# The remainder product of the attention scores: 64 partitions, or 128 with zeros in half of them

## The chip, the cores and the metric

The kernel runs on one core of a Trainium2 chip. What counts is the time of one execution on the device, in microseconds (us); lower is better. Before the change three executions took 495.58, 497.87 and 500.51 us, the median being 497.87 us.

## What is computed

One decoder layer in float32 on 256 tokens of 1024 channels. The part that matters here is the attention. There are two kinds, with heads of 64 channels: 12 dilated heads in three groups, and 8 block heads. For each head the scores are a product of queries and keys over the 64 channels of that head:

```python
sc = jnp.einsum('brhnqd,brhnkd->brhnqk', qb, kb).astype(jnp.float32) * scale   # dilated
s_own = jnp.einsum('bhqd,bhnd->bhqn', qc, ko).astype(jnp.float32) * scale      # block (256 tokens: one block)
p = softmax(masked scores);  o = p @ v
```

Around the attention stand large products with weights: an input projection of 1024 by 8448 columns, gates, branch projections, an output projection, and a feed-forward part of 2816 hidden channels. Two layer norms end the two halves.

## The kernel before

**Numbers in two parts.** TensorE multiplies float32 numbers here in a form that is rounded to fewer bits (`float32r`). Each operand is therefore split into a rounded part and a remainder, and a product is the sum of three matmuls: part by part, part by remainder, remainder by part (`mm3`, lines 198 to 202). The splitting is done by `split` (lines 148 to 150): ScalarE (ACT) casts, VectorE (DVE) subtracts. The weights go through it too: `prep` (line 129) takes pieces of 128x512 that a DMA has brought in and splits each, up to 10 pieces (`LEAD`) ahead of their use.

**The order.** The main thread is a run of projections. `project` (line 209) does two tiles of 128 channels, each a sum of 24 matmuls of 128x256 in a bank of PSUM. After each tile `tick` (line 155) splits further weights, takes the product out of its bank, and takes one entry from the list `side`. An entry of `side` is one stage of an attention: scores, exponentials, transposes, values. So TensorE meets a burst of score matmuls every few ticks between the matmuls of projections, and keeps its program order throughout.

**Queries and keys.** Heads go in pairs, head a of a pair at partitions 64a to 64a+63 of a tile. `queries` (line 233) stores for head a the rounded part on its own half of the partitions and the remainder on the other half, so that one tile of 128 partitions holds both. `keys` (line 244) stores the rounded part of the keys twice, once on each half (the tile `k`); a first matmul over 128 partitions then gives part by part plus remainder by part in one go (line 265). The remainder of the keys lies only on the head's own half (the tile `kl`, one for two pairs of heads, made at line 246 and filled at line 257). A second matmul over these 64 partitions (line 266) adds part by remainder to the same bank.

**How many.** A score is those two matmuls for one head and one tile of 128 queries by 256 keys. A dilated stage (`score`, line 316) does six scores, and there are four such stages. A block stage (`score`, line 360) does four, and there are four of these too. That makes 40 scores, 80 matmuls, in eight bursts. The DVE reads the finished scores at line 273, ACT takes the exponentials at line 275, DVE normalizes at line 280, and the results are transposed on TensorE at line 287.

**Buffers.** Nearly all tiles of 128x512 come from one pool with 61 slots (`buf`, line 57). GpSimd (POOL) does almost nothing: an iota at the start and four tiny powers in the layer norms.

Of the kernel before, what the change touches and what calls it, by code (L numbers as in the profile page):

```python
# [7 lines left out]
F32 = mybir.dt.float32  # L8
F32R = mybir.dt.float32r
# [5 lines left out]
P = 128  # L15
# [22 lines left out]
def trunk(ctx: ExitStack, tc, x, w_in, w_short_conv, w_moba_proj, w_dil_proj, w_conv_proj, w_mix_out,  # L38
# [26 lines left out]

    # ---- the stream of weights: blocks of up to [128, 2048] are loaded, and in pieces of 512 columns
    # ---- rounded to the tensor engine's 12-bit form, with the remainder
    blocks = []

    def block(*parts):  # L70
        """parts: DRAM access patterns [128, k, columns], one behind the other in the block"""
        blocks.append(parts)
# [56 lines left out]
    def prep(n=1):  # L129
        """the next n pieces, as far as they may run ahead"""  # L130
        for _ in range(n):
            i = len(ready)
            if i >= min(len(pieces), used[0] + LEAD):
                return
            r, c, last = pieces[i]
            h, l = buf(F32R), buf(F32R)
            split(r[:, c:c + 512], h, l)
            ready.append((h, l))
            if last:
                load_next()  # L140

    def take(n):
        """the next n pieces"""
        i = used[0]
        assert len(ready) >= i + n, (len(ready), i, n)
        return ready[i:i + n]
# [4 lines left out]

    # ---- work set between the products that hold the tensor engine
    side, late = [], []

    def tick(n, consume=None, ahead=1):
        """after n pieces' worth of products: what the last time left, more weights, what takes these
        products, and a stage of the work that is set between"""
        used[0] += n
        while late:
            late.pop(0)()  # L160
        prep(n + ahead)
        if consume:
            consume()
        if side:
            side.pop(0)()

    # ---- the tensor engine's clock is raised while the first loads are under way
    warm = const.tile([P, 512], BF16, name="warm")
# [4 lines left out]

    # ---- x, and its transpose
    xs = act.tile([P, 2, D], F32, tag="xs", name="xs", bufs=2)
# [20 lines left out]

    # ---- products
    def mm3(o, ah, al, bh, bl, first, last):
        """o += (ah + al)' (bh + bl), all but the product of the two remainders (2^-24)"""
        nc.tensor.matmul(o, ah, bh, start=first, stop=False)  # L200
        nc.tensor.matmul(o, ah, bl, start=False, stop=False)  # L201
        nc.tensor.matmul(o, al, bh, start=False, stop=last)  # L202

    def cut(w, k, c0, c1):
        """rows k, columns c0..c1 of a block of 256 columns in pieces w"""
        c = (k % 2) * 256
        return [t[:, c + c0:c + c1] for t in w[k // 2]]

    def project(consume, xh=xTh, xl=xTl, ahead=1):
        """[128 channels, 256 tokens] for two tiles of channels; consume(tile, product)"""  # L210
        w = take(4)
        for c in range(2):
            o = acc((P, T))
            for k in range(KT):
                mm3(o, *cut(w, k, c * P, c * P + P), xh[:, k, :], xl[:, k, :], k == 0, k == KT - 1)
            tick(2, lambda: consume(c, o), ahead)

    def project_tokens():
        """tokens by 256 channels, in two parts: [128 tokens, 2, 256 channels]"""
        w = take(4)  # L220
        vh, vl = buf(F32R, (P, 2, 256)), buf(F32R, (P, 2, 256))
        for t in range(2):
            s = slice(t * P, (t + 1) * P)
            o = acc((P, T))
            for k in range(KT):
                mm3(o, xTh[:, k, s], xTl[:, k, s], *cut(w, k, 0, 256), k == 0, k == KT - 1)
            tick(2, lambda: split(o, vh[:, t, :], vl[:, t, :]))
        return vh, vl

    # ---- attention: heads go in pairs, head a of a pair at partitions 64 a  # L230
    HALF = (slice(0, 64), slice(64, 128))

    def queries(store):
        """per tile of two heads: [part and remainder of a head, 2 heads, 256 tokens]"""
        def consume(c, o):
            q = buf(F32R, (P, 2, T))
            for a in range(2):
                s, n = HALF[a], HALF[1 - a]
                nc.scalar.copy(q[s, a, :], o[s, :])
                nc.vector.tensor_sub(q[n, a, :], o[s, :], q.bitcast(F32)[s, a, :])  # L240
            store.append(q)
        return consume

    def keys(store):
        """per tile: the part of a head, twice [128, 2 heads, 256 tokens]; the remainders [128, 256]"""
        kl = buf(F32R, (P, 2, T))

        def consume(c, o):
            k = buf(F32R, (P, 2, T))
            for a in range(2):  # L250
# [4 lines left out]
                else:  # L255
                    nc.vector.tensor_copy(k[n, a, :], o[s, :])
                nc.vector.tensor_sub(kl[s, c, :], o[s, :], k.bitcast(F32)[s, a, :])
            store.append((k, kl[:, c, :]))
        return consume

    def scores(o, q, k, a, t):
        """o [128 queries of tile t, 256 keys] for head a of a pair"""
        kd, kl = k
        ts = slice(t * P, (t + 1) * P)
        nc.tensor.matmul(o, q[:, a, ts], kd[:, a, :], start=True, stop=False)  # L265
        nc.tensor.matmul(o, q[HALF[a], a, ts], kl[HALF[a], :], start=False, stop=True)  # L266

    def exponentials(e, parts):
        """parts: (part of e, scores in PSUM, mask); e = exp((s + mask) / 8 - max); returns its sums"""
        n = len(parts)  # L270
# [11 lines left out]
    def turned(blks):  # L282
        """transposes of up to four [128, 128] tiles, split: two of [128, 4, 128]"""
        n = len(blks)
# [11 lines left out]
    def values(vs, ps, c):  # L296
        """vs: per group (vh, vl); ps: per group the transposed probabilities of keys 0..127 and 128..255"""
        o = att((P, 2, T))
# [13 lines left out]
    def dilated(c, dq, dk, dv, y):  # L312
        """the stages of a pair of heads, the three groups in one softmax"""
        es, ps, en = {}, {}, []
# [73 lines left out]

    # ---- masks (additive), by shape alone
    mask1 = const.tile([P, 3, 2, P], F32, name="mask1")  # L390
# [12 lines left out]

    # ---- small per-channel weights, turned to columns
    sconv = const.tile([P, 3, 4], F32, name="sconv")
# [22 lines left out]

    # ---- the mixer's projections and attention
    dq, dk, dv = [[], [], []], [[], [], []], []  # L430
# [71 lines left out]

    # ---- gates and branch projections
    merged = []
# [25 lines left out]

    # ---- layer norm
    half_c = const.tile([P, 1], F32, name="half_c")
    nc.vector.memset(half_c, -0.5)

    def residual(r, res, o, st, i, c0, c1):
        """columns c0..c1 of r = ALPHA res + o, with their statistics"""
        nc.vector.scalar_tensor_tensor(r[:, c0:c1], res[:, c0:c1], ALPHA, o, op0=OP.mult, op1=OP.add)
        nc.vector.bn_stats(st[:, i, :], r[:, c0:c1])

    def norm(r, st, gB, bB, ends, done=lambda c0, c1: None):  # L540
        """over r, in parts of columns that end at ends; done(first column, last)"""
        mv = act.tile([P, 4], F32, tag="mv", name=fresh("mv"), bufs=2)
# [11 lines left out]
    def row_products(o, a, w, k, t, c0, c1, first, last):  # L554
        """o += columns c0..c1 of row k of a block of 1024 columns, in pieces w, by the tokens of tile t"""
        ah, al = (v[:, k, t * P:(t + 1) * P] for v in a)
# [3 lines left out]
    def sums():  # L560
        """banks of the sums of the two token tiles by parts of the columns: (first column, last, sum)"""
        res = []
# [4 lines left out]
    def finish(o, t, parts, r, res, between=lambda: None):  # L567
        """the last products of token tile t, in parts of columns that end one after the other, and the
        residual sum; parts: (activations, pieces of the weights)"""
        st = act.tile([P, len(o), 6], F32, tag="bn", name=fresh("bn"), bufs=2)  # L570
# [12 lines left out]

    # ---- output projection of the mixer, tokens by channels
    x1 = act.tile([P, 2, D], F32, tag="xs", name="x1", bufs=2)
# [37 lines left out]

    # ---- gated feed-forward with a causal convolution
    def taps(v, o, ch):
# [5 lines left out]
    def hidden(j):  # L631
        """the consumers of the two halves of w_up, and what they give"""
        vg, vv = buf(F32, (P, 2, T)), buf(F32, (P, 2, T))
# [98 lines left out]
```

## Time and profile before

| what | value |
|---|---|
| time of three executions | 495.58, 497.87, 500.51 us |
| median | 497.87 us |
| span of the profiled execution, first to last instruction | 493.7 us |
| TensorE matmul busy | 483.7 us (98%) |
| VectorE busy | 361.6 us (73%) |
| ScalarE busy | 271.9 us (55%) |
| GpSimd busy | 4.3 us (1%) |

The profiled execution is another one than the three that were timed, and the only time that its records hold is its span of 493.7 us. The times of executions without the profiler stand 1.8 to 6.8 us above that span, the median 4.1 us. The timeline gives for each instruction its start and its duration. The matmuls overlap one another in a pipeline, so what one of them costs in a run of them is not its duration but the distance from its start to the start of the next.

### The profile page before, as it was taken

The numbers are of one execution on the slowest core, as the hardware profiler recorded it, in microseconds if no ns is written. First come the engines' busy times: TensorE is split into PE (matmuls) and PEld (weight loads), VectorE is DVE, ScalarE is ACT, GpSimd is POOL, SyncE is SP. The second block draws the span as 40 slices with busy tenths as digits, with TensorE's granted clock in tenths as the row PEclk, the third lists the DMA queues.
The fourth block names the chain that finished last, engine by engine and source line by source line (L and its number), as shares of the span: only waits on it lengthen the run. The fifth ranks groups of instructions, "written<-read, shape, count | busy, mean of one in ns | idle before, by whom it ended". The sixth has DMA issues, their size and how long they took to land.

```text
span 493.7 us, 9076 instructions
## 1 busy us (share of the span) xinstructions
PE 483.7 (98%) x3582; PEld 457.3 (93%) x3582; DVE 361.6 (73%) x775; ACT 271.9 (55%) x579; POOL 4.3 (1%) x9
## 2 busy tenths in 40 slices
PE   8999999999999999999999999999999999999993
PEld 5999788999899999999999889999999999999983
DVE  6888768476788865656565986798677867776966
ACT  4768455364756673535353712876655646565710
POOL 0000000000000000000000000000000000000000
PEclk9999899999999999999999999999999999999997
DMA  8975535353435163737374843546656374556102
GB/s 265 362 233 175 167 96 161 86 170 106 152 110 169 39 217 108 242 122 244 119 254 174 276 151 129 214 157 212 229 175 216 124 251 173 166 178 195 61 1 86
DMA packets 69502, 83.51 MB, mean 169 GB/s; under 512 B 1688, under 2 KB 64852, under 8 KB 69460
## 3 DMA queue, kind: packets, MB, share of 16 engines
q1 hardware_dynamic: 69460, 82.94, 51.4%
q8 instruction: 28, 0.46, 0.4%
q14 instruction: 14, 0.11, 0.1%
HBM read 81.89 MB, written 1.05 MB: 168 GB/s over the span
## 4 chain that ended last, share of the span: by engine, by line
PE 97%; DMA 1%; DVE 1%; SPq 0%; ACT 0%; issue 0%; DVEq 0%
PE acc L200 23%; PE acc L202 23%; PE acc L201 23%; PE att L200 6%; PE att L201 6%; PE att L202 6%; PE att L266 3%; PE att L265 2%; PE att L287 1%; PE acc L439 1%; DMA xs<-in_x_dram 1%; PE att L194 0%; DVE r L551 0%; SPq L124 0%; SPq L177 0%
## 5 line engine op out<-in xcount | busy, mean ns | idle before, releaser
L150 DVE TENSOR_TENSOR b<-raw,b 128x512 fp32r<-128x512 f32 x300 | 196.4, 686 | 39.6 <-ACT b L149 36.5
L149 ACT CAST b<-raw 128x512 fp32r<-128x512 f32 x300 | 169.6, 620 | 6.9 <-DMA raw<-in_w_in_dram 3.9
L200 PE MATMUL acc<-xTh,b 128*128 128x256 f32 x432 | 123.3, 285 | 0.0
L201 PE MATMUL acc<-xTl,b 128*128 128x256 f32 x432 | 122.2, 283 | 0.0
L202 PE MATMUL acc<-xTh,b 128*128 128x256 f32 x432 | 122.2, 283 | 0.0
L200 PE MATMUL acc<-x1Th,b 128*128 128x256 f32 x320 | 90.9, 284 | 0.0
L202 PE MATMUL acc<-x1Th,b 128*128 128x256 f32 x320 | 90.6, 283 | 0.0
L201 PE MATMUL acc<-x1Tl,b 128*128 128x256 f32 x320 | 90.5, 283 | 0.0
L200 PEld LDWEIGHTS acc<-xTh,b 128*128 128x128 f32 x432 | 82.8, 192 | 0.7
L201 PEld LDWEIGHTS acc<-xTl,b 128*128 128x128 f32 x432 | 82.8, 192 | 0.0
L202 PEld LDWEIGHTS acc<-xTh,b 128*128 128x128 f32 x432 | 82.8, 192 | 0.0
L201 PEld LDWEIGHTS acc<-x1Tl,b 128*128 128x128 f32 x320 | 61.4, 192 | 0.1
L200 PEld LDWEIGHTS acc<-x1Th,b 128*128 128x128 f32 x320 | 61.4, 192 | 0.1
L202 PEld LDWEIGHTS acc<-x1Th,b 128*128 128x128 f32 x320 | 61.4, 192 | 0.0
L629 DVE SCALAR_TENSOR_TENSOR b<-acc,fconv,b 128x255 f32<-128x255 f32 x80 | 38.4, 480 | 30.2 <-ACT b L627 29.2
L200 PE MATMUL att<-b,b 128*128 128x512 f32 (+1 forms) x170 | 58.9, 347 | 0.0
L201 PE MATMUL att<-b,b 128*128 128x512 f32 (+1 forms) x170 | 58.9, 347 | 0.0
L202 PE MATMUL att<-b,b 128*128 128x512 f32 (+1 forms) x170 | 58.7, 345 | 0.0
L149 ACT CAST b<-b 128x256 fp32r<-128x256 f32 x34 | 13.8, 408 | 47.3 <-DVE b L525 23.4
L627 ACT ACTIVATE b<-acc,fconv 128x256 f32<-128x256 f32 x40 | 22.6, 564 | 28.7 <-PE acc L202 28.6
L200 PEld LDWEIGHTS att<-b,b 128*128 128x128 f32 x170 | 32.2, 189 | 4.0
L202 PEld LDWEIGHTS att<-b,b 128*128 128x128 f32 x170 | 32.1, 189 | 4.0
(109 smaller groups left out, 646.6 us busy)
## 6 DMA issues: line engine op xcount, KB each, us to landing
raw<-in_w_in_dram SPq DMA_DIRECT2D x31, 1024.0 KB, 5.7
raw<-in_w_up_dram SPq DMA_DIRECT2D x22, 1024.0 KB, 5.1
raw<-in_w_down_dram SPq DMA_DIRECT2D x11, 1024.0 KB, 5.1
raw<-in_w_mix_out_dram SPq DMA_DIRECT2D x4, 1024.0 KB, 5.1
raw<-in_w_in_dram SPq DMA_DIRECT2D x8, 256.0 KB, 6.0
raw<-in_w_conv_proj_dram SPq DMA_DIRECT2D x4, 512.0 KB, 3.6
raw<-in_w_moba_proj_dram SPq DMA_DIRECT2D x4, 512.0 KB, 4.6
xs<-in_x_dram SPq DMA_DIRECT2D x4, 256.0 KB, 3.5
```

The costliest lines, as they stand in the source:

```text
L149: nc.scalar.copy(h, src)
L150: nc.vector.tensor_sub(l, src, h.bitcast(F32))
L200: nc.tensor.matmul(o, ah, bh, start=first, stop=False)
L201: nc.tensor.matmul(o, ah, bl, start=False, stop=False)
L202: nc.tensor.matmul(o, al, bh, start=False, stop=last)
L265: nc.tensor.matmul(o, q[:, a, ts], kd[:, a, :], start=True, stop=False)
L266: nc.tensor.matmul(o, q[HALF[a], a, ts], kl[HALF[a], :], start=False, stop=True)
L287: nc.tensor.transpose(p[:, i, :], b, ident)
L439: nc.tensor.matmul(o[c], w[i][:, s:s + P], xt[:, k, :], start=k + i == 0 and xt is xTh, stop=k == KT - 1 and i == 1)
L627: nc.scalar.activation(v, o, AF.Identity, bias=w[3], scale=w[0])
L629: nc.vector.scalar_tensor_tensor(v[:, j:], o[:, :T - j], w[j], v[:, j:], op0=OP.mult, op1=OP.add)
```

## The change

`keys` makes a tile of remainders for each pair of heads (`kl`, now inside `consume`) in the same layout as the tile of parts: for head a, the remainder lies on that head's half of the partitions, and GpSimd writes zeros on the other half. `scores` runs both matmuls over all 128 partitions with the same stationary operand. Over the zeros, the rows that hold the remainder of the queries add nothing. The rest of the diff takes comments and doc strings away, so the line numbers stay nearly the same.

```diff
     def keys(store):
-        """per tile: the part of a head, twice [128, 2 heads, 256 tokens]; the remainders [128, 256]"""
-        kl = buf(F32R, (P, 2, T))
+
 
         def consume(c, o):
-            k = buf(F32R, (P, 2, T))
+            k, kl = buf(F32R, (P, 2, T)), buf(F32R, (P, 2, T))
+            for a in range(2):
+                nc.gpsimd.memset(kl.bitcast(F32)[HALF[1 - a], a, :], 0.0)
             for a in range(2):
                 s, n = HALF[a], HALF[1 - a]
                 nc.scalar.copy(k[s, a, :], o[s, :])
@@ -254,19 +255,18 @@
                     nc.scalar.copy(k[n, a, :], o[s, :])
                 else:
                     nc.vector.tensor_copy(k[n, a, :], o[s, :])
-                nc.vector.tensor_sub(kl[s, c, :], o[s, :], k.bitcast(F32)[s, a, :])
-            store.append((k, kl[:, c, :]))
+                nc.vector.tensor_sub(kl[s, a, :], o[s, :], k.bitcast(F32)[s, a, :])
+            store.append((k, kl))
         return consume
 
     def scores(o, q, k, a, t):
-        """o [128 queries of tile t, 256 keys] for head a of a pair"""
-        kd, kl = k
-        ts = slice(t * P, (t + 1) * P)
-        nc.tensor.matmul(o, q[:, a, ts], kd[:, a, :], start=True, stop=False)
-        nc.tensor.matmul(o, q[HALF[a], a, ts], kl[HALF[a], :], start=False, stop=True)
+
+        qt = q[:, a, t * P:(t + 1) * P]
+        for i in range(2):
+            nc.tensor.matmul(o, qt, k[i][:, a, :], start=i == 0, stop=i == 1)
```

## Rows read from the trace of the kernel before

**Rows 1.** The page's first part: span, and for engines the busy time, share of the span and number of instructions.

```profile
span 493.7 us, 9076 instructions
...
PE 483.7 (98%) x3582; PEld 457.3 (93%) x3582; DVE 361.6 (73%) x775; ACT 271.9 (55%) x579; POOL 4.3 (1%) x9
```

**Rows 2.** The page's chain of work that ended last, followed back from the last instruction: shares of the span by engine, then by line.

```profile
PE 97%; DMA 1%; DVE 1%; SPq 0%; ACT 0%; issue 0%; DVEq 0%
PE acc L200 23%; PE acc L202 23%; PE acc L201 23%; PE att L200 6%; PE att L201 6%; PE att L202 6%; PE att L266 3%; PE att L265 2%; PE att L287 1%; PE acc L439 1%; DMA xs<-in_x_dram 1%; PE att L194 0%; DVE r L551 0%; SPq L124 0%; SPq L177 0%
```

**Rows 3.** The view of who waited for whom, PE alone: us in total, times, longest.

```profile
PE att L194 <- DMA xs<-in_x_dram: 1.2, 2, 0.8
PE acc L172 <- DVE warm L169: 1.2, 1, 1.2
```

**Rows 4.** The timeline of PE around the burst of four block scores at 126.56 us: start, duration, line, rows*columns of the array, shape of the moving operand.

```profile
126.20 0.28 PE L200 MATMUL acc<-xTh,b 128*128 128x256 f32 x1
126.33 0.28 PE L201 MATMUL acc<-xTl,b 128*128 128x256 f32 x1
126.44 0.28 PE L202 MATMUL acc<-xTh,b 128*128 128x256 f32 x1
126.56 0.28 PE L265 MATMUL att<-b,b 128*128 128x256 f32 x1
126.77 0.38 PE L266 MATMUL att<-b,b 64*128 64x256 f32 x1
127.08 0.39 PE L265 MATMUL att<-b,b 128*128 128x256 f32 x1
127.40 0.38 PE L266 MATMUL att<-b,b 64*128 64x256 f32 x1
...
128.65 0.38 PE L266 MATMUL att<-b,b 64*128 64x256 f32 x1
128.96 0.39 PE L200 MATMUL acc<-xTh,b 128*128 128x256 f32 x1
129.19 0.28 PE L201 MATMUL acc<-xTl,b 128*128 128x256 f32 x1
```

**Rows 5.** The timeline of PEld, the loads of the stationary operand, over the same burst.

```profile
126.45 0.19 PEld L265 LDWEIGHTS att<-b,b 128*128 128x128 f32 x1
126.77 0.18 PEld L266 LDWEIGHTS att<-b,b 64*128 64x128 f32 x1
127.08 0.19 PEld L265 LDWEIGHTS att<-b,b 128*128 128x128 f32 x1
```

**Rows 6.** The timeline of PE at the transposes of the small weights, with 12 and 44 rows.

```profile
33.23 0.44 PE L425 MATMUL att<-ident,b 44*128 44x44 f32 x4
33.61 0.39 PE L200 MATMUL acc<-xTh,b 128*128 128x256 f32 x1
33.83 0.28 PE L201 MATMUL acc<-xTl,b 128*128 128x256 f32 x1
```

**Rows 7.** Eight stretches, each from the first score matmul of a burst to the next matmul of a projection: the stretch and its length; busy time of PE (and how many instructions touch the stretch, those that began before it included), granted clock, DMA share, GB/s.

```profile
48.10:51.95 3.85, 3.85 (x15) 0.93 0.70 209
56.17:59.82 3.65, 3.65 (x14) 1.00 0.69 241
65.69:69.34 3.65, 3.65 (x15) 1.00 0.92 282
80.03:83.67 3.64, 3.64 (x15) 1.00 0.54 133
126.57:128.96 2.39, 2.39 (x10) 1.00 0.46 108
131.93:134.32 2.39, 2.39 (x10) 1.00 0.00 0
157.95:160.35 2.40, 2.40 (x11) 1.00 0.33 109
163.31:165.71 2.40, 2.40 (x11) 1.00 0.00 0
```

**Rows 8.** Stretches of 1 us at the end of the first burst and behind it: busy time of PE, PEld, DVE, ACT and POOL with their counts, granted clock (1.00 is 2.4 GHz, 0.50 is 1.2 GHz), DMA share, GB/s.

```profile
51.00:52.00 1.00, 1.00 (x4) 0.53 (x3) 0.97 (x5) 0.81 (x1) 0.00 (x0) 0.70 1.08 385
52.00:53.00 1.00, 1.00 (x6) 1.00 (x6) 0.91 (x4) 1.00 (x4) 0.00 (x0) 0.50 0.69 225
53.00:54.00 1.00, 1.00 (x6) 1.00 (x6) 0.88 (x2) 0.34 (x2) 0.00 (x0) 0.50 0.00 0
54.00:55.00 1.00, 1.00 (x8) 1.00 (x7) 0.00 (x0) 0.00 (x0) 0.00 (x0) 0.59 0.02 6
```

**Rows 9.** GpSimd's groups of instructions: shapes and count, busy time, mean ns of one.

```profile
L545 POOL TENSOR_TENSOR mv<-mv,half_c 128x1 f32<-128x1 f32 x4 | 3.8, 955 | 483.8 <-DVE mv L544 483.8
L183 POOL IOTA diff<- 128x128 int32 x1 | 0.2, 236 | 0.4 <-POOLq L719 0.4
L719 POOL MEMSET const-float32-0.0<- 128x1 f32 x1 | 0.1, 99 | 0.2 <-issue 0.2
```

**Rows 10.** Four longer stretches in the form of rows 8: the projections of the keys, the four dilated bursts, the stretch behind them, and the block attention.

```profile
30.00:48.00 18.00, 18.00 (x152) 17.79 (x151) 16.31 (x34) 13.70 (x32) 0.00 (x0) 1.00 0.61 185
48.00:84.00 36.00, 36.00 (x215) 29.71 (x214) 27.34 (x74) 19.73 (x45) 0.00 (x0) 0.95 0.45 134
84.00:120.00 36.00, 36.00 (x288) 35.22 (x287) 22.73 (x47) 17.33 (x39) 0.00 (x0) 1.00 0.42 130
120.00:180.00 60.00, 60.00 (x444) 55.35 (x443) 48.54 (x142) 39.32 (x103) 0.00 (x0) 1.00 0.38 120
```

**Rows 11.** The view of who waited for whom, the DVE's wait for finished scores.

```profile
DVE e L273 <- PE att L266: 7.2, 11, 2.3
```

**Rows 12.** The timeline of the DVE as it splits the last transposed probabilities of the first block stage.

```profile
139.79 0.42 DVE L150 TENSOR_TENSOR b<-att,b 128x256 fp32r<-128x256 f32 x1
```

**Rows 13.** The timeline of PE as it uses them in the values of that stage.

```profile
141.50 0.28 PE L200 MATMUL att<-b,b 128*128 128x256 f32 x1
141.62 0.28 PE L201 MATMUL att<-b,b 128*128 128x256 f32 x1
```

**Rows 14.** The timeline of the DVE in the projections of the keys: two pieces of weights split, and the subtractions that make the remainders of keys for the first pair of heads of the third group.

```profile
40.89 1.27 DVE L150 TENSOR_TENSOR b<-raw,b 128x512 fp32r<-128x512 f32 x2
...
43.39 0.42 DVE L257 TENSOR_TENSOR b<-acc,b 64x256 fp32r<-64x256 f32 x1
...
44.63 0.43 DVE L257 TENSOR_TENSOR b<-acc,b 64x256 fp32r<-64x256 f32 x1 [0.22 <-ACT b L254]
```

## The prediction

> **What bounds the kernel now.** I read the page's busy shares first, then its chain of work, then PE's own waits. TensorE is busy for 483.7 of 493.7 us, with the DVE at 73% and GpSimd at 1% [rows 1]. Busy time alone proves little where matmuls overlap, but the chain agrees: 97% of what ended last is PE, nearly all of it the three matmuls of `mm3`, and about 5% is lines 265 and 266 [rows 2]. PE waited for another engine for only 2.4 us, all of it at the start [rows 3]. So between about 10 us and the last layer norm TensorE runs from one matmul to the next, and a microsecond less of its own time is a microsecond less in all, as long as its operands still come in time.
>
> Next I read the timeline inside one burst of scores [rows 4]. What counts is the distance between starts. Before the burst, matmuls over 128 rows start 0.12 us apart (126.20, 126.33, 126.44, 126.56). In it, the distance is 0.21 us to the first matmul over 64 rows and then 0.31 to 0.32 us at every step. The step is as long from 64 to 128 rows as from 128 to 64, although line 265 has the shape of line 200 (128x256, over 128 rows). The first projection matmul behind the burst pays too (128.65 to 128.96, and 0.23 more to its successor), and then 0.12 returns. The loads of the stationary operand show how it comes about [rows 5]: line 265's first load starts 0.11 us before its matmul, under the running one, but from line 266 on each load starts only together with its own matmul's turn (126.77, 127.08), so nothing overlaps across a change between 64 and 128 rows. A second place has such a change without scores: behind the transposes over 44 rows, line 200 starts 0.22 us ahead of line 201 [rows 6]. So the cost belongs to the change of rows, not to the scores.
>
> **The change, part by part.**
>
> *The matmuls.* It removes every change of rows in the bursts. The count of matmuls and loads stays at 80. The eight bursts take 3.85 + 3.65 + 3.65 + 3.64 + 2.39 + 2.39 + 2.40 + 2.40 = 24.37 us [rows 7]. A matmul over 128 rows with 256 columns between others of its kind costs 0.12 us [rows 4], and 80 of them 9.60 us. Gain: 24.37 - 9.60 = 14.8 us. The bounds: 0.12 is what 128 rows by 256 columns show everywhere in the projections; the nearest worse row is the 0.21 us between line 265 and the first line 266, which would leave 80 x 0.21 = 16.8 us and a gain of 7.6. I take 0.12, since the new line 266 has the form of lines 200 to 202 in every respect that the rows show.
>
> The Trainium skill, TensorE: Matmul & The Clock Gate, section Part 3 (What overlaps and what doesn't), states that a weight load overlaps a running matmul only if it goes to another row group; by that rule two matmuls over the same 128 rows could not hide their loads, and the gain would be the 7.6 us above. The trace speaks against it here: lines 200 to 202 all use 128 rows, each with a load of its own, and still start 0.12 us apart.
>
> *The clock.* Behind the first burst, the longest stretch of slow steps, the granted clock falls to 1.2 GHz: 0.70, 0.50, 0.50 and 0.59 in four stretches of 1 us, and line 200 and its followers run at that level before the clock returns [rows 8]. The clock lost is 0.30 + 0.50 + 0.50 + 0.41 = 1.71 us. Of this 0.20 lies inside the first burst already (3.85 against 3.65 [rows 7]), so 1.5 us come on top. With dense bursts TensorE does not slow down there and I expect no fall. The bounds are 0 (it falls all the same) and 1.5; I take 1.5.
>
> *The zeros.* Ten tiles of keys get two memsets each: 20, each over 64 partitions by 256 columns. The trace has none of that size. From below, a memset of one column takes 0.10 us; an iota of 128 columns takes 0.24, from which 0.10 + 2 x 0.14 = 0.37 us is an estimate for 256 columns; the dearest row of GpSimd, the power, takes 0.96 [rows 9]. So 2 to 19 us, most likely under 7.4, on an engine that is idle for 99% of the span and has nothing queued behind them. They need neither the product nor the cast and go ahead of both. Line 266 also waits for them, but far later. If the cover were gone, the DVE's subtraction (line 257) would wait, with splits of weights behind it. Twelve of the memsets fall into the projections of the dilated keys, where the DVE is busy for 16.31 of 18.00 us [rows 10]. At 0.37 that is 4.4 us against 1.7 idle, 2.7 late; the pieces split at 40.89 to 42.16 us [rows 14] are used by PE at 46.78 and 47.50 (counted through the program's order), a lead of about 5 us. It holds. At 0.96, 11.5 us less 1.7 less 5.2 leaves a wait of 4.6 us. I take 0 and keep 4.6 as the far end.
>
> The Trainium skill, GPSIMD Engine Reference, section Key points, says that GpSimd shares its SBUF interfaces with the VectorE and contends with instructions with two SBUF inputs, which the splits are. Its page SBUF — State Buffer, in the list on contention, limits that to GpSimd instructions that read, and a memset only writes. No row here shows the two at once. By the first page the 2.7 us late above would come about; by the second nothing.
>
> *The added tiles.* Three more tiles live through the dilated attention. Counted in program order, at most 51 of the 61 slots are in use at once; 54 leaves the pool free of waits. The subtractions keep their shape, 64x256. Nothing is added to ACT, the DMA queue or SP.
>
> **What the others make of it.** From 48 to 84 us TensorE gets ahead by 14.79 - 48 x 0.12 + 1.5 = 10.5 us. The DVE is idle for 36.00 - 27.34 = 8.7 us there [rows 10], so it falls behind by at most 1.9, within the lead of weights, and finds 13.3 idle us behind it. From 120 to 180 us TensorE gains 9.58 - 32 x 0.12 = 5.7, and the DVE has 11.5 idle. The DVE even gets time back: 7.2 us of its idle time is waiting for the burst's matmuls themselves [rows 11]. The tightest place is the values of a block stage: a split ends at 140.21 us [rows 12] and is used at 141.62 [rows 13], 1.4 us of slack, while two bursts ahead of it shrink by 2.9. If the DVE recovered nothing, that would be 1.5 us of waiting, twice: 3.0. It recovers most of it, so I take 0.5 in all. The first burst asks for the remainders of the third group at its sixth matmul, 48.10 + 5 x 0.12 = 48.7 us; they end at 45.06 [rows 14].
>
> **The sum.** 493.7 - 14.8 - 1.5 + 0.5 = 477.9 us for a profiled execution. The three times shown stand 1.8, 4.1 and 6.8 us above the span of 493.7. Part of that may be falls of the clock behind other bursts in those executions (each 1.7 us), which would go too. I therefore add 3.0, between the lowest and the median: **481.0 us**, 3.4% below the median of 497.87.
>
> **The rivals.**
>
> *TensorE outruns the DVE* (8%). For it: the DVE is at 76% and 81% of the two stretches now [rows 10], and would come near all of them. Against it: up to ten pieces of lead and idle time behind both. It would show as waits of PE on lines 149 and 150. Price: 1.9 + 3.0 = 4.9 us of waits, so 477.4 + 4.9 + 3.0 = 485.3 us, and 4.6 more with the dearest memsets, 489.9.
>
> *Loads do not overlap with the same rows* (3%), the skill's rule above. For it: in the burst no load overlaps now. Against it: rows 4. Gain 7.6 + 1.5; 477.4 + 7.2 + 3.0 = 487.6 us.
>
> *The rows are not the cause* (2%), for example because both matmuls use the same stationary tile. Then the bursts stay at 0.31 and the time at 497.9. Against it: rows 6, and line 200 behind each burst.
>
> *The memsets hold up the DVE* (2%), the one that ends slower. A memset waits until the slot of its tile is given back, the subtraction into the same tile waits for the memset, and every split behind it on the DVE's queue too. It decides only from 1.6 us per tile of keys on TensorE (16.3 us over 10 tiles), beyond a lead of 5 us: some 7 us of wait in a tile. With 5 us more than the gain, 503 us. Against it: seven slots stay free.
>
> **How the numbers follow.** The forecast has 85%: bursts at 0.12, no or one fall of the clock, waits up to 3 us. A measurement of this kernel can tell about 1% from no change, 5 us. Faster by more than that (under 492.9): 85 + 8 + 3 = 96%; within it 2%; slower 2%. The range from the bounds: 477.4 without any wait at no offset at all is its low end, 477.5; the high end is 477.4 + 1.9 + 3.0 + 4.1 (the median's offset) = 486.4, rounded to 486.5, which takes in most of the first rival. About 1 in 10 lies above, fewer below, and the offsets of the runs take the rest.
>
> **What would show it.** Line 266 in the form 128*128, with starts 0.12 us apart in all eight bursts: 1.44 us for twelve matmuls, 0.96 for eight. Line 200 behind a burst at the pace of its followers. A granted clock of 1.00 from 51 to 55 us. Twenty memsets on POOL under 0.4 us each, without a DVE wait on them at line 257. PE's waits still under 3 us. I am wrong if the bursts keep steps of 0.2 us or more, or if PE waits for lines 149, 150 or 257 behind the bursts.

## The result, and the profile after

| | before | after |
|---|---|---|
| median, us | 499.19 (495.58 to 500.59, 4 runs) | 478.85 (478.23 to 480.43, 4 runs) |
| ratio after / before | | 0.9637, 95% interval 0.9591 to 0.9683 |
| span of the profiled execution, us | 493.7 | 477.5 |

By the ratio on record the change makes the kernel 3.6% faster; the two medians alone would give 4.1%. The forecast was 481.0 us, with a range of 477.5 to 486.5, and 477.9 us for the profiled span. The rest of this section reads the trace after the change, beside the groups of rows shown ahead of the prediction.

The page's first part and its chain of work, which answer to [rows 1, 2]:

```profile
span 477.5 us, 9121 instructions
...
PE 466.5 (98%) x3582; PEld 450.6 (94%) x3582; DVE 360.3 (75%) x775; ACT 271.0 (57%) x579; POOL 10.4 (2%) x29
...
PE 97%; DMA 1%; DVE 1%; SPq 0%; ACT 0%; issue 0%; DVEq 0%
```

TensorE lost 17.2 us of busy time with the same number of matmuls, and it is still the whole chain. The DVE's work is the same to 1.3 us, in a shorter span. Twenty instructions are new on POOL.

The timeline of PE at the first block burst, which answers to [rows 4]. A row with x8 merges eight matmuls of one form:

```profile
116.20 0.28 PE L201 MATMUL acc<-xTl,b 128*128 128x256 f32 x1
116.32 0.28 PE L202 MATMUL acc<-xTh,b 128*128 128x256 f32 x1
116.44 1.12 PE L266 MATMUL att<-b,b 128*128 128x256 f32 x8
117.40 0.28 PE L200 MATMUL acc<-xTh,b 128*128 128x256 f32 x1
117.52 0.28 PE L201 MATMUL acc<-xTl,b 128*128 128x256 f32 x1
```

From the first score matmul to the next projection matmul it is 117.40 - 116.44 = 0.96 us for eight, 0.12 each, where it was 2.39 us [rows 7]. The successor of line 200 follows after 0.12 us, not 0.23. The chain of work in order of time shows all eight bursts alike, twelve matmuls in 1.44 us and eight in 0.96; four of its pieces:

```profile
48.81 1.44 PE att L266 x12
53.13 1.44 PE att L266 x12
...
116.60 0.96 PE att L266 x8
...
148.79 0.96 PE att L266 x8
```

Together that is 4 x 1.44 + 4 x 0.96 = 9.60 us in place of 24.37, so 14.8 us, as the sum had it.

The clock and the load of the engines around the first burst and from there on, in the columns of [rows 8]:

```profile
44.00:60.00 16.00, 16.00 (x136) 16.00 (x135) 15.40 (x44) 12.32 (x29) 0.00 (x0) 1.00 0.61 197
60.00:80.00 20.00, 20.00 (x162) 19.61 (x161) 18.25 (x48) 12.88 (x30) 0.00 (x0) 1.00 0.52 161
80.00:120.00 40.00, 40.00 (x329) 39.61 (x328) 28.29 (x65) 22.90 (x55) 1.23 (x4) 1.00 0.48 150
120.00:180.00 60.00, 60.00 (x494) 59.48 (x493) 48.30 (x131) 38.80 (x96) 1.23 (x4) 1.00 0.43 138
```

The granted clock stays at 1.00 through all of the attention. The DVE is now busy for 15.40 of 16.00 us around the first burst (96%), close to its limit, and TensorE still never stands idle. The waits of PE, and the DVE's wait for scores that answers to [rows 11]:

```profile
PE att L194 <- DMA xs<-in_x_dram: 2.3, 2, 1.6
PE acc L172 <- DVE warm L169: 1.2, 1, 1.2
...
DVE e L273 <- PE att L266: 0.6, 2, 0.4
```

PE waits for nothing but the start. The 7.2 us that the DVE spent waiting for scores have become 0.6, and that is how it keeps up.

The start is where this execution did worse than the one of before: x came later (2.3 us of waiting against 1.2 [rows 3]), and while TensorE stood still its clock fell. Two of the stretches of 1 us that show it:

```profile
7.00:8.00 1.00, 0.12 (x1) 0.12 (x2) 1.00 (x2) 0.38 (x1) 0.00 (x0) 0.95 0.90 266
8.00:9.00 1.00, 1.00 (x5) 1.00 (x6) 0.18 (x1) 0.00 (x0) 0.00 (x0) 0.50 0.99 312
```

The first score matmul therefore starts at 48.65 us, 0.55 later than before (48.10). From there to the end of the last burst it is 149.59 - 48.65 = 100.9 us, where it was 165.71 - 48.10 = 117.6: a gain of 16.7 us, of which the start takes 0.55 back.

The memsets on POOL, which answer to [rows 9]:

```profile
L250 POOL MEMSET b<- 64x256 f32 x20 | 6.2, 310 | 121.1 <-PE att L202 71.9 <-PE acc L201 27.4 <-PE acc L439 10.8
```

One takes 0.31 us, and no DVE instruction waits on one. A split of weights takes 687 ns on average, and took 686 before.

### The profile page after: what moved, and what is told of

The parts are those of the page before. It is cut to its first block, busy times and chain, and to the rows that moved or that the text cites. A ratio compares the mean times of both kernels' runs of the same rounds, so it can differ in the third digit from the quotient of the medians.

```text
span 477.5 us, 9121 instructions
## 1 busy us (share of the span) xinstructions
PE 466.5 (98%) x3582; PEld 450.6 (94%) x3582; DVE 360.3 (75%) x775; ACT 271.0 (57%) x579; POOL 10.4 (2%) x29
## 4 chain that ended last, share of the span: by engine, by line
PE 97%; DMA 1%; DVE 1%; SPq 0%; ACT 0%; issue 0%; DVEq 0%
PE acc L200 24%; PE acc L202 24%; PE acc L201 24%; PE att L201 7%; PE att L200 7%; PE att L202 7%; PE att L266 2%; PE acc L439 1%; PE att L287 1%; DMA xs<-in_x_dram 1%; PE att L194 0%; DVE r L551 0%; SPq L124 0%; SPq L177 0%; PE acc L594 0%
```

## The experiments

The times of the kernel before in these runs, 23 executions, are 494.68 to 501.32 us with a median of 497.31, unless another number is given.

**The rows alone.** The kernel before, with one line changed. It leaves out the product with the remainder of the keys and adds the product of the first matmul a second time.

```diff
-        nc.tensor.matmul(o, q[HALF[a], a, ts], kl[HALF[a], :], start=False, stop=True)
+        nc.tensor.matmul(o, q[:, a, ts], kd[:, a, :], start=False, stop=True)
```

> The kernel before, but the second matmul runs over all 128 partitions of the tile of key parts again, in place of the remainders, so the product with the remainder of the keys is left out (part by part is added twice); no memsets, no added tiles. If the change of rows is all of the gain, the bursts run at 0.12 us a step and the time is that of the changed kernel, 478.9 us within 1.5. If the zeros and the new tiles do something of their own, for good or ill, it differs from the changed kernel by more than that.

Measured: 478.31 us (478.14 to 479.36, 4 runs), ratio 0.962 (0.9572 to 0.9668). Span 476.4 us. That is the changed kernel's time without memsets and without a new tile, so the form of the matmul brings the whole gain.

**The zeros alone.** The changed kernel, with the second matmul over 64 partitions as before.

```diff
-            nc.tensor.matmul(o, qt, k[i][:, a, :], start=i == 0, stop=i == 1)
+        nc.tensor.matmul(o, q[:, a, ts], k[0][:, a, :], start=True, stop=False)
+        nc.tensor.matmul(o, q[HALF[a], a, ts], k[1][HALF[a], a, :], start=False, stop=True)
```

> The changed kernel with its memsets and its tiles of remainders, but the second matmul over the 64 partitions of the head again, as before. If the change of rows is all of the gain, this is the kernel before, 496 to 500 us, with steps of 0.31 us in the bursts. If the memsets cost anything that the gain hid, it is slower than before by that: up to 4.6 us by the dearest row of GpSimd.

Measured: 497.17 us (495.5 to 498.94, 10 runs), ratio 1.0003 (0.9974 to 1.0032). The memsets and the three tiles cost nothing that can be measured.

**64 rows kept, changes of rows taken out.** In each burst all first matmuls, then all second ones; the cut shows the dilated bursts, and the block bursts are changed alike. (The bank's first matmul alone carries the start flag, so that the second region of the bank keeps its sum.)

```diff
+            for i in range(2):
+                for n, (o, g, t) in enumerate(((x[:, 0, :], 0, 1), (x[:, 1, :], 1, 1), ...
+                    scores(o, q[g], k[g], a, t, i, n % 2 == 0)
...
```

> The kernel before with its matmuls over 64 partitions kept, but in each burst all first matmuls (128 rows) stand ahead of all second ones (64 rows), so that a burst changes rows twice and not after every matmul: 16 changes in place of 80. Theory, the cost lies in the change of rows: about 0.19 us for each of 16 changes is left, 3 of 14.8 us, so bursts of 1.8 and 1.3 us, and a gain of about 12 us and the 1.5 of the clock: some 482 us. Rival, a matmul over 64 rows is itself slow because its load of the stationary operand can't be hidden: the 40 of them keep 0.31 us, bursts of 2.6 and 1.7 us, and a gain of 7 us: some 488 us.

Measured: 480.65 us, the median of three executions (479.78, 480.65 and 480.91). A fourth took 921.09 us, with a span of 919.3 us at a mean granted clock of 1.00; no trace of it was kept, and why it took so long stays open. Ratio of the three 0.9656 (0.9608 to 0.9704). The timeline of PE at the first burst (line 266 is here the matmul over 128 rows, line 268 the one over 64):

```profile
48.13 0.28 PE L202 MATMUL acc<-b,xTl 128*128 128x256 f32 x1
48.25 0.88 PE L266 MATMUL att<-b,b 128*128 128x256 f32 x6
49.06 0.97 PE L268 MATMUL att<-b,b 64*128 64x256 f32 x6
49.96 0.38 PE L200 MATMUL acc<-b,xTh 128*128 128x256 f32 x1
50.19 0.28 PE L201 MATMUL acc<-b,xTh 128*128 128x256 f32 x1
```

The loads of the stationary operand at the same place (PEld):

```profile
48.13 0.79 PEld L266 LDWEIGHTS att<-b,b 128*128 128x128 f32 x6
49.06 0.77 PEld L268 LDWEIGHTS att<-b,b 64*128 64x128 f32 x6
49.96 0.19 PEld L200 LDWEIGHTS acc<-b,xTh 128*128 128x128 f32 x1
```

The burst takes 49.96 - 48.25 = 1.71 us, against 3.65 with the changes at every step and 1.44 without any. Six matmuls over 64 rows start on average 0.15 us apart, the change back included, and the six loads, 0.18 us each alone, fit into 0.77 us: among themselves they overlap as those over 128 rows do. Only the first load of each form still starts together with its matmul (49.06, 49.96). So 64 rows are not slow in themselves. The rival (488 us) is out. The two changes cost 1.71 - 1.44 = 0.27 us in the burst, and behind it the successor of line 200 follows after 50.19 - 49.96 = 0.23 us in place of 0.12. That is 0.38 us for two changes, 0.19 each, as much as a change costs at every step of the kernel before.

The four block bursts lose less than that. The timeline of PE at the first of them:

```profile
117.51 0.64 PE L266 MATMUL att<-b,b 128*128 128x256 f32 x4
118.08 0.51 PE L268 MATMUL att<-b,b 64*128 64x256 f32 x4
118.52 0.38 PE L200 MATMUL acc<-xTh,b 128*128 128x256 f32 x1
118.74 0.28 PE L201 MATMUL acc<-xTl,b 128*128 128x256 f32 x1
```

This burst takes 1.01 us against 0.96 without changes, and the successor of line 200 pays its 0.1 us as before. But the four matmuls over 64 rows take only 118.52 - 118.08 = 0.44 us, since they start in two pairs, with 0.01 us between the two of a pair. Two of the four lie on each half of the rows; the six of a dilated burst all lie on one half, and behind the first they start 0.12 us apart. That a pair is made of the two halves is argued from this, since the records do not name the half. So the eight bursts are left with 4 x 0.38 + 4 x 0.15 = 2.1 us, where the expectation had 3.

**Which bursts.** The second matmul over 128 rows only in the dilated bursts, or only in the block bursts; one flag to `scores`:

```diff
+        h = slice(0, P) if full else HALF[a]
+        nc.tensor.matmul(o, q[h, a, ts], k[1][h, a, :], start=False, stop=True)
```

> The changed kernel, but the second matmul of the 16 block scores runs over 64 partitions again; the 24 dilated scores stay at 128. Theory: what is given back is the excess of the four block bursts alone, 4 x (2.39 - 0.96) = 5.7 us on 478.4, so 484.1. If the clock falls only behind the long dilated bursts (3.65 us), where the two falls seen so far stood, none is seen here and the executions lie within 2.5 us of one another, as those of the changed kernel do. Rival: the DVE takes part of the gain of the block bursts back already, and then less than 5.7 us is lost, say 3.

> The reverse: the 24 dilated scores over 64 partitions, the 16 block scores over 128. Theory: the excess of the four dilated bursts comes back, 14.79 - 5.76 = 9.0 us on 478.4, so 487.4 in an execution without a fall of the clock behind them, and 1.7 more for each fall: a median of 488 to 491 and a spread of some 4 us or more. If falls come from the rest of the kernel, the spread is that of the run with dilated scores over 128.

Measured, against 497.69 us of before (9 runs): with only the dilated ones at 128 rows 485.39 us (484.37 to 486.22), span 483.1; with only the block ones 490.38 us (489.03 to 492.91), span 487.4. The span of the first is 5.6 us above that of the changed kernel's profiled execution, for 5.7 expected, but the fit is partly luck: the four block bursts give 4 x (2.39 - 0.96) = 5.7 us and the slow successors behind them 4 x 0.1, and the start of this execution lay 0.5 us earlier (first score matmul at 48.13 us, where it was 48.65). So the DVE had taken nothing of the loss back. The medians are 6.5 us apart; the spans of the four executions vary by 1.8 us and those of the changed kernel by 2.2, in which the 0.4 us that the bursts do not explain lie. The second run shows the larger loss and, as expected, the larger spread: 3.9 us against 1.9. Its profiled execution had no fall behind a burst, and its two slowest executions have a mean clock of 0.981 and 0.986, the two fastest 0.993 and 0.996; that falls make its spread is argued from this.

**How executions of the kernel before differ.** It was run unchanged five more times with a profile.

> The kernel before, unchanged, to see how its executions differ from one another. If falls of the clock behind bursts of scores explain the spread of 495.6 to 500.6 us, the slower executions show a lower granted clock, each fall of 3.4 us at 1.2 GHz costing 1.7 us and 0.0035 of the mean clock (1.7 of 494): an execution at 500.6 would have three falls more than one at 495.6, and a clock of about 0.981 against 0.991. If something else makes the spread, time and clock go apart.

Measured in the first of these runs: twelve executions took 495.02 to 500.97 us, and the mean clock goes with the time, as expected, over a wider range than the 0.981 to 0.991 put down: it is 0.993 to 0.997 in the four under 495.4 us and 0.977 in the three above 500.6 us.

> The kernel before once more, for the records of one execution. If falls of the clock make the spread, the time of the execution follows their number: with f falls (counted in the granted clock, and at the start in the spacing of the matmuls) about 494 + 1.7 f us, so 495.7 with one and 499 with three.

The other three (e8b, e8c and e8d) carried the same expectation. The windows of 4 us behind the dilated bursts, e8b:

```profile
56.00:60.00 4.00, 4.00 (x14) 2.78 (x15) 3.41 (x13) 2.18 (x6) 0.00 (x0) 0.71 0.61 215
60.00:64.00 4.00, 4.00 (x20) 4.00 (x20) 1.75 (x5) 0.57 (x2) 0.00 (x0) 0.50 0.00 0
64.00:68.00 4.00, 4.00 (x29) 3.61 (x28) 1.12 (x2) 2.09 (x5) 0.00 (x0) 0.93 0.19 19
68.00:72.00 4.00, 4.00 (x18) 2.84 (x18) 3.63 (x11) 1.69 (x5) 0.00 (x0) 0.92 0.70 243
72.00:76.00 4.00, 4.00 (x25) 4.00 (x25) 1.62 (x6) 1.69 (x6) 0.00 (x0) 0.65 0.27 43
```

and e8c:

```profile
64.00:68.00 4.00, 4.00 (x14) 2.39 (x13) 2.86 (x10) 1.60 (x4) 0.00 (x0) 0.90 0.83 261
68.00:72.00 4.00, 4.00 (x25) 4.00 (x26) 2.29 (x6) 1.96 (x5) 0.00 (x0) 0.68 0.17 16
```

The clock lost there is 4 x (0.29 + 0.50 + 0.07 + 0.08 + 0.35) = 5.2 us in e8b and 4 x (0.10 + 0.32) = 1.7 us in e8c. Read in the same way for all six:

| execution of the kernel before | time, us | span, us | clock lost behind bursts, us | span less that, us |
|---|---|---|---|---|
| shown ahead of the prediction | 495.58 | 493.7 | 1.7 | 492.0 |
| e1 | 495.36 | 493.6 | 1.7 | 491.9 |
| e8a | 497.26 | 495.5 | 3.4 | 492.1 |
| e8b | 498.44 | 496.7 | 5.2 | 491.5 |
| e8c | 495.13 | 493.4 | 1.7 | 491.7 |
| e8d | 495.91 | 494.1 | 1.7 | 492.4 |

Without these falls the six executions agree within 0.9 us, so the falls make most of their spread. They all lie behind dilated bursts, at one or two places in an execution (the first of e8b lasts twice as long as the others), and which ones differs. Read from the starts of the matmuls, 3.4 us at 1.2 GHz delay what follows by 1.4 to 1.5 us, a little less than the 1.7 that the clock alone gives. What is left then is the start: the first score matmul starts at 47.75 to 48.43 us, and from there to the end each of the six takes 444.2 us and the delays of its falls. The time follows the number of falls behind bursts. The falls at the start, which the expectation counted too, cost at most 0.7 us in these six, so as it was put down it misses two: e8a (499 us with three falls, measured 497.26) and e8d (497.4 with two, measured 495.91). The mean clock of a whole execution did not serve to count single falls: it is 0.988 for e8d and 0.994 for e8c, though both lost 1.7 us behind bursts, because it holds the start and the idle end too.

**Keeping the clock up at the start.** The changed kernel, with more matmuls on zeros between the groups of transposes of x.

```diff
     for k2 in range(KT // 2):
+        for i in range((0, 4, 6, 0)[k2]):
+            nc.tensor.matmul(wps, warm[:, :P], warm, start=True, stop=True)
         transpose_x(k2)
```

> The changed kernel, with 4 and 6 more matmuls on zeros ahead of the second and third group of transposes of x, where TensorE waits for x and where the profiled execution of the changed kernel lost its clock at 7.9 us. Theory: the added work lies in waiting time and costs nothing or up to 0.5 us; the fall at the start, 1.7 us in some executions, is gone: a median of 478 to 478.5 and no execution above 479. Rival: x comes in time in most executions and the added matmuls delay the transposes: 479 to 480.

Measured: 479.53 us (479.41 to 479.93, 5 runs), beside 478.85 for the changed kernel. A miss: the time is that of the rival. But its reason is not shown, because the timeline of PE shows another order than the one meant:

```profile
4.14 3.10 PE L444 MATMUL acc<-warm 128*128 128x512 bf16 x10
7.08 1.47 PE L194 MATMUL att<-ident,xs 128*128 128x128 f32 x12
9.11 0.66 PE L194 MATMUL att<-ident,xs 128*128 128x128 f32 x4 [0.56 <-DMA xs<-in_x_dram]
```

The ten matmuls were put in one row, ahead of all transposes, and not into the two gaps. The executions lie within 0.5 us of one another, and in the one traced the first score matmul starts at 49.08 us, later than in the changed kernel (48.65). Whether matmuls in the gaps themselves would keep the clock up stays untested.

## Why the prediction was right

**The steps in the bursts** (14.8 us) came out to the tenth, and [rows 4 to 6] were the right place to read them: the cost lies with the change of rows and not with the matmul over 64 rows. What was argued from line 200 behind a burst is now shown by the grouped order, which keeps all 40 matmuls over 64 rows and still saves most of the time. The Trainium skill, TensorEngine Tiling (Array Packing), section Key Properties, says that changing the tiling mode drains the TensorE; the traces agree: a load does not go ahead across such a change, and the change costs 0.19 us, at every step where each matmul is a change and no less where a burst has only two.

**The rule against it** failed here: by the Trainium skill, TensorE: Matmul & The Clock Gate, Part 3, loads to the same row group would not have overlapped, and the bursts would have stayed at 0.21 us a step. They run at 0.12.

**The clock** behind the bursts stayed up, as expected, but the fall had cost less than the 1.5 us of the sum. From the end of the first burst to the start of the second it was 56.17 - 51.95 = 4.22 us [rows 7]; where no fall lies between them it is 2.97 (e1). So 1.25 us came on top of the 0.20 inside the burst.

**The term that was left out** is the slow successor of line 200. The prediction read it (0.23 us in place of 0.12), but its sum ends each burst at line 200. It is worth 0.1 us behind each burst, 0.7 for the seven ahead of the last burst's end. 14.8 + 1.25 + 0.7 give the 16.7 us gained between the first score matmul and the end of the last burst.

**The waits** were taken at 0.5 us and are 0. The tight place of [rows 12, 13] is as tight as it was: the split ends at 126.63 + 0.42 = 127.05 and is used at 128.45 us, again 1.4 us apart.

```profile
126.63 0.42 DVE L150 TENSOR_TENSOR b<-att,b 128x256 fp32r<-128x256 f32 x1
```

```profile
128.45 0.28 PE L201 MATMUL att<-b,b 128*128 128x256 f32 x1
```

That the span came within 0.4 us of the forecast is therefore partly luck: the successors (0.8 us) and the waits (0.5) made it shorter than the sum, the clock (0.25) and the start (0.55) longer.

**The zeros** were taken at nothing and cost nothing; one memset takes 0.31 us, where the estimate was 0.37. Nine of the 300 splits of weights ran while a memset did; they took 681 to 693 ns, and the others 687 on average, so the lateness worked out for the case that the two engines contend did not come about.

**The step that was mis-sized** is the last one, from the span to the time without the profiler: 3.0 us were added, between the lowest of the three times and their median. It is 1.7 to 1.8 us in every execution here, of either kernel (497.26 against 495.5, 479.29 against 477.5). By this the profiled execution of before is not another one than the three that were timed, as was said ahead of the prediction, but, as far as the times tell, the one of 495.58 us. The rest of what was seen as an offset was in the main falls of the clock, which the change takes away with the steps. That is also why the medians differ by 18 to 20 us and the two spans by 16.2: the profiled execution of before had one fall, and the median of 497.31 us, 5.3 us above the 492.0 of a span without falls, has room for the 1.8 and for two. How many falls an execution without records had is argued from its time, not shown.

## What to carry to other kernels

In a run of TensorE matmuls look at the distances between starts, not at durations: a matmul that uses fewer rows than its neighbours is as long as they are, but makes the engine wait twice, going in and coming back, here 0.19 us each time. Fill the rows with zeros, or put the matmuls of one form together; here the first is worth 14.8 us inside the bursts and the second nearly as much. And where executions of one kernel spread by more than 1%, look at the granted clock in stretches of a few us before calling it noise: a slow stretch can cost a second time behind it.

## What was not expected of the hardware

In all six traced executions of the kernel before the clock fell to 1.2 GHz behind dilated bursts of 3.65 us, for 3.4 us once in four of them, twice in e8a and three times in e8b (two of these in one go), and never behind block bursts of 2.4 us. It did not fall there at all with bursts at 0.12 us a step. Nor did it in the two other traces with dilated bursts of 3.65 us, those of the zeros alone and of block scores at 128 rows, so such a burst can bring a fall and need not; what decides stays open. The granted clock of the profile does not show all of the start: in the run with the zeros alone, the windows give 1.00 from 10 to 12 us, while eight matmuls take 1.91 us, which take 1.12 us in the run with dilated scores at 128 rows. The run with block scores at 128 rows has a row of 1.91 us there too, and in these two runs the first score matmul starts at 49.81 and 49.29 us. Whether the clock had fallen or had not yet risen is not shown. Two rows of PE, each from its own run:

```profile
10.99 1.91 PE L439 MATMUL acc<-xTh,b 128*128 128x256 f32 x8
```

```profile
10.57 1.12 PE L440 MATMUL acc<-xTh,b 128*128 128x256 f32 x8
```
